# Attention of a two-layer trunk: low weight parts made by adding transfers, softmax weights transposed on row halves

## The chip, the cores and the metric

The kernel runs on one core of a Trainium2 chip. The metric is the time on the device of one execution, in microseconds; times before and after are medians of several runs. The engines are named as in the profile: PE (TensorE) with its weight loads PEld, DVE (VectorE), ACT (ScalarE), POOL (GpSimd) and SP (SyncE, which issues most transfers).

## The reference

Two layers work on 256 latent tokens and 256 context tokens, each with 1024 channels, in float32. What matters here is the token-mixing half of a layer:

```python
h  = modulate(rmsnorm(x,  norm1_g[l]), sh1,  sc1)      # latent
hc = modulate(rmsnorm(xc, norm1_g[l]), csh1, csc1)     # context
p  = h @ w_in[l]       # conv branch | q | k | v | gates
pc = hc @ w_in[l]      # in the last layer only its k and v
q, k = rope_2d(q), rope_2d(k)
y_conv = conv_branch(p[..., :GLU_END], ...)            # GLU, 31 taps, LayerNorm, swish, projection
s = concat(window scores + bias, context scores)       # 8 heads of 64
y_attn = (softmax(s) @ [v_win, v_ctx]) @ w_na_out[l]
x = x + g1 * gated_merge(p[..., QKV_END:], y_conv, y_attn, w_out[l])
```

In the first layer the context tokens go through the same steps and attend to context alone. A gated MLP with a convolution of width 3 follows in each layer, and the output is the latent stream after a last RMSNorm.

## The kernel before

Activations lie with channels on the 128 partitions and tokens along the free dimension: 512 columns (latent, context) in the first layer, 256 in most of the second. To keep float32 accuracy with TensorE's faster float32r type, every operand is split into a high part, rounded to float32r, and a low part, the rest. A product is then three matmuls (`mm3`, L179 to L181): high weight by high activation, high weight by low activation, low weight by high activation. The low part of a weight is needed only by the third.

Weights come in units of 128 x 1024 numbers (512 KB), eight 128 x 128 blocks each. `wunit` loads a unit into a `raw` buffer by a transfer that SP issues (L157), ACT copies it to `whi` (L160), and DVE subtracts the two into `wlo` (L161). `raw`, `whi` and `wlo` have four buffers each, so a unit can be made ready while three others wait or are in use. `unit8` returns a unit as eight pairs for `group`, which makes one output tile of 128 channels from eight blocks, that is 24 matmuls.

In the first layer the order of units in the input projection is: queries and keys of head pair 0 (units 6 and 10 of `U_IN`), then for each of the pairs 1 to 3 two units of the convolution's GLU and the pair's queries and keys, then gates from unit 14 on. In the second layer GLU units 0 and 1 come first, then four units of values, units 2 and 3, the first pair, 4 and 5, and then gates alternate with the other pairs.

Attention runs beside this. `group` calls `slot`, and a slot lets side work take a step: convolution taps on DVE, and `Attention.step`. A step does up to three things in PE's order: `turn` transposes the softmax weights that the step before left (16 transposes of 128 x 128; L494 for latent queries, L499 for context ones) and has ACT copy each of four PSUM banks to `pT` (L495, L500); `values` multiplies `V` with an earlier `pT` (L512); `products` makes the next scores (L440), on 64 rows of the array for each of the two heads of a pair. DVE then adds bias and takes the maximum (L458), and ACT does the exponential and the scaling (L461, L464). PSUM banks come under the names `sc` (two), `pt`, `po` and `main` (four); a turn and the scores after it use the same `sc`, `pt` and `main`.

The engines run their queues in order. The order in each queue is fixed when the program is built, from program order and when data and buffers are expected; `issue_after` adds orders by hand.

Of the kernel before, what the change touches and what calls it, by code (L numbers as in the profile page):

```python
# [8 lines left out]
F32 = mybir.dt.float32  # L9
F32R = mybir.dt.float32r  # L10
BF16 = mybir.dt.bfloat16
AF = mybir.ActivationFunctionType
ALU = mybir.AluOpType
AX = mybir.AxisListType

P = 128
# [3 lines left out]
S = 256  # L20
# [11 lines left out]
UW = 1024  # L32
LAT, CTX = slice(0, S), slice(S, 2 * S)
# [3 lines left out]

U_GLU0, U_V, U_IN, U_NA, U_CO, U_WO, U_UP, U_DN = 0, 2, 6, 36, 40, 44, 52, 96
NU = 118
T_GLU, T_Q, T_K, T_GATE = 0, 6, 10, 14  # L40

SWAP16 = [(i + 16) % 32 for i in range(32)]
# [3 lines left out]
def trunk(ctx: ExitStack, tc: tile.TileContext, xt, cvec, crow, wall, wada, params, bias_t, rope_t, out):  # L46
    nc = tc.nc
# [12 lines left out]
    def nm(s):  # L60
        uid[0] += 1
        return f"{s}_{uid[0]}"
# [3 lines left out]
    def psum(tag="main"):  # L66
        return psp.tile([P, 512], F32, tag=tag, bufs=BANKS[tag], name=nm(tag))
# [7 lines left out]
    def sl(w, i):  # L75
        return w[:, i * P : (i + 1) * P]
# [29 lines left out]
    start = ExitStack()  # L106
# [38 lines left out]
    def raw_unit(src, r=None):  # L145
        r = wp.tile([P, UW], F32, tag="raw", bufs=4, name=nm("raw")) if r is None else r
        lastdma[0] = sp.dma_start(r, src)
        return r
# [21 lines left out]
    def wunit(l, u, at=None, cuts=1):  # L170
        w, more = wparts(l, u, at, cuts)
        more()
        return w
# [9 lines left out]
    def group(ps, ws, xh, xl, c):  # L183
# [6 lines left out]
        slot()  # L190
        return ps

    def unit8(l, u, at=None):
        w = wunit(l, u, at)
        return [cols(w, i) for i in range(KD)]


# [187 lines left out]
    class Attention:  # L385
# [99 lines left out]

        def turn(self, what, its, pps):

            pts = [self.eb.tile([P, 4, S], F32, tag="pT", bufs=4, name=nm("pT")) for _ in range(2)]
            for n, tags in enumerate((("sc", "sc"), ("pt", "main"))):
                for i, pp in enumerate(pps[n]):  # L490
                    pt = psum(tags[i])
                    if what == LAT:
                        for kt in range(4):
                            pe.transpose(sl(pt, kt), sl(pp, kt), ident)  # L494
                        act.copy(pts[i][:, :, n * P : (n + 1) * P], pt.rearrange("p (k q) -> p k q", k=4))  # L495
                    else:
                        for t in range(2):
                            for kt in range(2):
                                pe.transpose(pt[:, kt * S + t * P : kt * S + (t + 1) * P], sl(pp, 2 * t + kt), ident)  # L499
                        act.copy(pts[i][:, 2 * n : 2 * n + 2, :], pt.rearrange("p (k q) -> p k q", k=2))  # L500
            js = [its[0][0]] if what == LAT else [it[0] for it in its]
            self.pv.append((what, js, pts))

        def values(self, what, js, pts, bank):
            po = psum(bank)
            kts = range(4) if what == LAT else range(2, 4)
            for n, j in enumerate(js):
                c = slice(n * S, (n + 1) * S)
                for kt in kts:
                    for i in range(2):  # L510
                        h = 2 * j + i
                        pe.matmul(  # L512
                            po[i * HD : (i + 1) * HD, c], self.V[kt][:, h * HD : (h + 1) * HD],
                            pts[i][:, 2 * n + kt - kts[0], :], start=kt == kts[0], stop=kt == kts[-1],
                        )
            for n, j in enumerate(js):
                c = slice(n * S, (n + 1) * S)
                act.copy(self.oh[j][:, what], po[:, c])
                dve.tensor_tensor(self.ol[j][:, what], po[:, c], self.oh[j][:, what].bitcast(F32), ALU.subtract)
# [705 lines left out]
```

## Time and profile before

| | |
|---|---|
| median of 3 runs | 1127.9 us (1127.66 to 1128.62) |
| the profiled execution | 1127.64 us, span 1125.9 us |
| granted TensorE clock, mean | 0.998 |
| PE busy | 1114.1 us (99%) |
| PEld busy | 963.0 us (86%) |
| DVE busy | 908.3 us (81%) |
| ACT busy | 563.6 us (50%) |
| POOL busy | 14.7 us (1%) |

The attention of the first layer lies between about 82 and 199 us, that of the second between 797 and 867 us. A timeline line gives start in us, duration in us, engine, line, operation, the tile written and those read, the shape and how often it was merged; in square brackets stands idle time of the engine before it and what ended it. For matmuls the start-to-start distance is the pace; the durations overlap.

### The profile page before, as it was taken

To read this page: it belongs to the slowest core of one execution; us is meant where nothing else is said; L and a number is where in the kernel's file an instruction comes from. 1 tells how busy PE (TensorE), PEld (TensorE's weight loads), DVE (VectorE), ACT (ScalarE), POOL (GpSimd) and SP (SyncE) were. 2 spreads that over 40 slices of the span, in tenths; PEclk is the share of its full clock that TensorE was granted. 3 is DMA by queue.
4 is the path that set the end of the run, shared out by engine and by line. 5 is a ranking of instruction groups with operands and counts; after the bars stand their busy time and mean duration, and the time that the engine had idled before them with its cause. 6 is when DMAs were issued, how large, how long until landed. Compare 5 with 4: busy or idle time off the path is not lost.

```text
span 1125.9 us, 17731 instructions
## 1 busy us (share of the span) xinstructions
PE 1114.1 (99%) x6828; PEld 963.0 (86%) x6828; DVE 908.3 (81%) x1631; ACT 563.6 (50%) x934; POOL 14.7 (1%) x24
## 2 busy tenths in 40 slices
PE   9999999999999999999999999999999999999997
PEld 7778777787789988888888888989888999999997
DVE  5689999685778788888898555789996898988773
ACT  4347657542333543434343222544677667766642
POOL 0000000000000000000000000000000000000000
PEclk9999999999999999999999999999999999999999
DMA  9833231536734354554556665556433575565781
GB/s 364 282 94 103 75 118 38 206 97 214 245 118 138 114 161 150 168 169 149 168 171 215 219 191 186 180 181 187 145 126 121 167 250 163 188 194 181 219 268 58
DMA packets 53941, 190.83 MB, mean 169 GB/s; under 512 B 6240, under 2 KB 6496, under 8 KB 53856
## 3 DMA queue, kind: packets, MB, share of 16 engines
q1 hardware_dynamic: 53568, 189.65, 52.1%
q8 instruction: 54, 0.88, 0.3%
q14 instruction: 31, 0.25, 0.1%
q10 hardware_dynamic: 288, 0.04, 0.0%
HBM read 188.62 MB, written 1.05 MB: 168 GB/s over the span
## 4 chain that ended last, share of the span: by engine, by line
PE 83%; DVE 9%; issue 6%; ACT 2%; DMA 0%; POOL 0%; POOLq 0%; DVEq 0%; SPq 0%; ACTq 0%
PE main L179 24%; PE main L181 24%; PE main L180 24%; DVE cb L591 4%; PE main L644 4%; DVE wlo L161 1%; PE sc L181 1%; PE sc L179 1%; PE sc L180 1%; PE po L202 1%; PE po L512 1%; PE sc L129 1%; PE sc L440 0%; DMA sb<-in_crow 0%; PE sc L494 0%
## 5 line engine op out<-in xcount | busy, mean ns | idle before, releaser
L179 PE MATMUL main<-h,whi 128*128 128x256 f32 (+1 forms) x1328 | 446.7, 337 | 0.0
L181 PE MATMUL main<-h,wlo 128*128 128x256 f32 (+1 forms) x1328 | 442.9, 335 | 1.0 <-DVE wlo L161 1.0
L180 PE MATMUL main<-h,whi 128*128 128x256 f32 (+1 forms) x1328 | 442.2, 334 | 0.1
L160 ACT CAST whi<-raw 128x1024 fp32r<-128x1024 f32 (+1 forms) x244 | 252.3, 1039 | 285.5 <-PE main L180 131.5
L161 DVE TENSOR_TENSOR wlo<-raw,whi 128x1024 fp32r<-128x1024 f32 (+1 forms) x244 | 292.9, 1207 | 112.5 <-ACT whi L160 108.0
L179 PEld LDWEIGHTS main<-h,whi 128*128 128x128 f32 x1328 | 249.4, 188 | 32.1 <-issue 3.6
L181 PEld LDWEIGHTS main<-h,wlo 128*128 128x128 f32 x1328 | 249.3, 188 | 29.6 <-DVE wlo L161 1.5
L180 PEld LDWEIGHTS main<-h,whi 128*128 128x128 f32 x1328 | 249.8, 188 | 28.5 <-DVE h L367 0.5
L591 DVE SCALAR_TENSOR_TENSOR cb<-u,par,cb 128x512 f32<-128x512 f32 (+1 forms) x240 | 140.4, 609 | 1.4
L271 DVE CUSTOM_DVE_ANT_0 t<-raw,sb,par 128x1024 bf16<-128x1024 f32 x100 | 126.7, 1277 | 1.0 <-ACT sb L255 0.7
L179 PE MATMUL main<-fh,whi 128*128 128x256 f32 (+1 forms) x386 | 123.0, 319 | 0.0
L180 PE MATMUL main<-fl,whi 128*128 128x256 f32 (+1 forms) x386 | 122.9, 319 | 0.0
L181 PE MATMUL main<-fh,wlo 128*128 128x256 f32 (+1 forms) x386 | 122.9, 318 | 0.0
L180 PEld LDWEIGHTS main<-fl,whi 128*128 128x128 f32 x386 | 72.7, 188 | 5.6
L179 PEld LDWEIGHTS main<-fh,whi 128*128 128x128 f32 x386 | 72.7, 188 | 5.6
L181 PEld LDWEIGHTS main<-fh,wlo 128*128 128x128 f32 x386 | 72.7, 188 | 5.5
L963 ACT ACTIVATE t<-main,par 128x512 f32<-128x512 f32 (+1 forms) x82 | 50.6, 667 | 39.0 <-PE main L181 39.0
L964 DVE SCALAR_TENSOR_TENSOR t<-main,par,t 128x510 f32<-128x510 f32 (+1 forms) x82 | 47.5, 615 | 10.2 <-ACT t L963 9.8
L967 DVE SCALAR_TENSOR_TENSOR t<-main,par,t 128x510 f32<-128x510 f32 (+1 forms) x82 | 46.6, 609 | 0.0
L366 ACT ACTIVATE h<-t,mod 128x256 fp32r<-128x256 f32 x56 | 25.4, 502 | 36.1 <-DVE t L365 36.1
L898 DVE SCALAR_TENSOR_TENSOR x<-main,mod,x 128x256 f32<-128x256 f32 x48 | 22.1, 479 | 23.5 <-PE main L181 23.3
L644 PE MATMUL main<-whi,h 128*128 128x512 f32 x128 | 40.6, 402 | 0.1
(221 smaller groups left out, 1188.2 us busy)
## 6 DMA issues: line engine op xcount, KB each, us to landing
raw<-in_wall SPq DMA_DIRECT2D x239, 512.0 KB, 4.2
raw<-in_wada SPq DMA_DIRECT2D x88, 512.0 KB, 4.3
bias<-in_bias_t SPq DMA_DIRECT2D x8, 640.0 KB, 4.8
row<-in_wada SPq DMA_DIRECT2D x8, 512.0 KB, 4.7
sb<-in_crow SPq DMA_DIRECT2D x5, 512.0 KB, 6.0
x<-in_xt SPq DMA_DIRECT2D x8, 256.0 KB, 4.4
raw<-in_wall SPq DMA_DIRECT2D x8, 256.0 KB, 7.1
out<-t SPq DMA_DIRECT2D x3, 256.0 KB, 2.1
```

What stands on the lines that cost most here:

```text
L160: act.copy(hi[:, c], r[:, c])
L161: dve.tensor_tensor(lo[:, c], r[:, c], hi[:, c].bitcast(F32), ALU.subtract)
L179: pe.matmul(ps, w[0], xh, start=start, stop=False)
L180: pe.matmul(ps, w[0], xl, start=False, stop=False)
L181: pe.matmul(ps, w[1], xh, start=False, stop=stop)
L271: dve.tensor_tensor_reduce(tmp().bitcast(BF16), r, v, 1.0, pr(l, BADA + n, 1), ALU.mult, ALU.add, mods[l][:, n, s : s + 1])
L366: high = act.activation(hi[:, c], y[:, c], AF.Identity, bias=b)
L591: dve.scalar_tensor_tensor(cb[j], src, w, cb[j], ALU.mult, ALU.add)
L644: mm = pe.matmul(pv[t], h1[n == 1][k][:, c], w[n == 2][:, b], start=k + n == 0, stop=k == KD - 1 and n == 2)
L963: act.activation(c, pv_, AF.Identity, bias=pr(l, FDB + t, 1), scale=w[1])
L964: dve.scalar_tensor_tensor(c[:, :, 1:], pv_[:, :, : S - 1], w[0], c[:, :, 1:], ALU.mult, ALU.add)
L967: dve.scalar_tensor_tensor(c[:, :, : S - 1], pv_[:, :, 1:], w[2], c[:, :, : S - 1], ALU.mult, ALU.add)
```

## The change

For 19 units of the first layer's input projection (0 to 18 of `U_IN`) and 11 of the second's (1, 3, 5 to 9 and 14 to 17), `unit8` calls `wadded` in place of `wunit`. There ACT makes the high part as before and then writes its negative into `wlo`; a transfer that GpSimd issues adds `raw` to it. DVE has no part in these units any more.

In `turn`, each 128 x 128 transpose becomes two: of rows 0 to 63 and of rows 64 to 127 of the weights. Each gives 64 columns, and the two go to two PSUM banks, so that one bank holds one half of the queries for both heads. Both banks of a pair are taken before the first transpose, and the two copies by ACT follow the 16 transposes of the pair. `pT` becomes one tile for both heads with as many bytes as the two before. For context the order of blocks inside the loop is rearranged so that one loop serves both kinds.

The space reserved for the descriptors of GpSimd's transfers is set to 1024 bytes per partition.

```diff
+ADDED = {*((0, U_IN + i) for i in range(19)), *((1, U_IN + i) for i in (1, 3, 5, 6, 7, 8, 9, 14, 15, 16, 17))}
...
+    def wadded(l, u):
+
+        r = raw_unit(wall[l, u])
+        hi = wp.tile([P, UW], F32R, tag="whi", bufs=4, name=nm("whi"))
+        lo = wp.tile([P, UW], F32R, tag="wlo", bufs=4, name=nm("wlo"))
+        act.copy(hi, r)
+        act.mul(lo, hi.bitcast(F32), -1.0)
+        pool.dma_start(lo, r, accum_op=ALU.add)
+        return hi, lo
+
     def unit8(l, u, at=None):
-        w = wunit(l, u, at)
+        w = wadded(l, u) if (l, u) in ADDED else wunit(l, u, at)
         return [cols(w, i) for i in range(KD)]
...
         def turn(self, what, its, pps):
 
-            pts = [self.eb.tile([P, 4, S], F32, tag="pT", bufs=4, name=nm("pT")) for _ in range(2)]
+            pT = self.eb.tile([P, 2, 4, S], F32, tag="pT", bufs=2, name=nm("pT"))
             for n, tags in enumerate((("sc", "sc"), ("pt", "main"))):
+                outs = [psum(t).rearrange("p (i s q) -> p i s q", i=2, s=4) for t in tags]
                 for i, pp in enumerate(pps[n]):
-                    pt = psum(tags[i])
+                    for s in range(4):
+                        src = s if what == LAT else s % 2 * 2 + s // 2
+                        for pt, r in zip(outs, HALF):
+                            pe.transpose(pt[:, i, s], sl(pp, src)[r], ident[r, r])
+                for pt, r in zip(outs, HALF):
                     if what == LAT:
-                        for kt in range(4):
-                            pe.transpose(sl(pt, kt), sl(pp, kt), ident)
-                        act.copy(pts[i][:, :, n * P : (n + 1) * P], pt.rearrange("p (k q) -> p k q", k=4))
+                        act.copy(pT[:, :, :, n * P + r.start : n * P + r.stop], pt)
                     else:
-                        for t in range(2):
-                            for kt in range(2):
-                                pe.transpose(pt[:, kt * S + t * P : kt * S + (t + 1) * P], sl(pp, 2 * t + kt), ident)
-                        act.copy(pts[i][:, 2 * n : 2 * n + 2, :], pt.rearrange("p (k q) -> p k q", k=2))
+                        to = pT[:, :, 2 * n : 2 * n + 2].rearrange("p i k (t q) -> p i (k t) q", t=2)
+                        act.copy(to[:, :, :, r], pt)
...
-                            pts[i][:, 2 * n + kt - kts[0], :], start=kt == kts[0], stop=kt == kts[-1],
+                            pT[:, i, 2 * n + kt - kts[0]], start=kt == kts[0], stop=kt == kts[-1],
...
-    nc = bacc.Bacc("TRN2", target_bir_lowering=False, num_devices=1)
+    nc = bacc.Bacc("TRN2", target_bir_lowering=False, num_devices=1, dynamic_dma_scratch_size=1024)
```

More of the change, by code (lines that the diff above doesn't have):

```diff
@@ L486, in turn, with values @@
         def turn(self, what, its, pps):
-            pts = [self.eb.tile([P, 4, S], F32, tag="pT", bufs=4, name=nm("pT")) for _ in range(2)]
+            pT = self.eb.tile([P, 2, 4, S], F32, tag="pT", bufs=2, name=nm("pT"))
             for n, tags in enumerate((("sc", "sc"), ("pt", "main"))):
+                outs = [psum(t).rearrange("p (i s q) -> p i s q", i=2, s=4) for t in tags]
                 for i, pp in enumerate(pps[n]):
-                    pt = psum(tags[i])
+                    for s in range(4):
[3 more added lines that the diff above has]
+                for pt, r in zip(outs, HALF):
                     if what == LAT:
-                        for kt in range(4):
-                            pe.transpose(sl(pt, kt), sl(pp, kt), ident)
-                        act.copy(pts[i][:, :, n * P : (n + 1) * P], pt.rearrange("p (k q) -> p k q", k=4))
-                    else:
-                        for t in range(2):
-                            for kt in range(2):
-                                pe.transpose(pt[:, kt * S + t * P : kt * S + (t + 1) * P], sl(pp, 2 * t + kt), ident)
-                        act.copy(pts[i][:, 2 * n : 2 * n + 2, :], pt.rearrange("p (k q) -> p k q", k=2))
+                        act.copy(pT[:, :, :, n * P + r.start : n * P + r.stop], pt)
+                    else:
+                        to = pT[:, :, 2 * n : 2 * n + 2].rearrange("p i k (t q) -> p i (k t) q", t=2)
+                        act.copy(to[:, :, :, r], pt)
             js = [its[0][0]] if what == LAT else [it[0] for it in its]
-            self.pv.append((what, js, pts))
-        def values(self, what, js, pts, bank):
+            self.pv.append((what, js, pT))
+        def values(self, what, js, pT, bank):
             po = psum(bank)
```

## The prediction

> **What bounds the kernel now.** I read the page's busy times first, then who waited for whom, then single stretches of the timeline.
>
> ```profile
> PE 1114.1 (99%) x6828; PEld 963.0 (86%) x6828; DVE 908.3 (81%) x1631; ACT 563.6 (50%) x934; POOL 14.7 (1%) x24
> ```
> ```profile
> PE main L181 <- DVE wlo L161: 1.0, 2, 0.6
> PE pt L1094 <- DVE t L314: 0.7, 1, 0.7
> ...
> PE pt L228 <- ACT t L221: 0.6, 1, 0.6
> ```
> ```profile
> 100.00:200.00 100.00, 100.00 (x572) 78.62 (x571) 99.46 (x191) 72.29 (x152) 2.99 (x2) 1.00 0.27 82
> 743.00:796.00 53.00, 53.00 (x315) 46.72 (x314) 52.93 (x115) 22.34 (x33) 0.00 (x0) 1.00 0.52 157
> ```
> The first row alone would not prove a PE bound, because matmul ends are modelled. The waits do: in the whole span PE waited 1.0 us for low parts (first of these rows: total, times, longest). The last two rows are the attention of the first layer and the start of that of the second; their columns are window, length, then busy us of PE, PEld, DVE, ACT, POOL, the granted clock (1.00), DMA share and GB/s. DVE is full there (99.46 of 100, 52.93 of 53), and yet PE has no idle time. So DVE is full without holding anything up: its low parts run far ahead of the matmuls that read them. Time can only be won here by shortening PE's own work.
>
> **The low parts.** Removed: 30 subtractions on DVE (19 in the first layer, 11 in the second). Added: 30 negated copies on ACT and 30 transfers issued by GpSimd.
>
> ```profile
> L161 DVE TENSOR_TENSOR wlo<-raw,whi 128x1024 fp32r<-128x1024 f32 x238 | 288.8, 1220 | 112.2 <-ACT whi L160 108.0 <-PE sc L181 3.2 <-PE sc L440 0.3
> ...
> L160 ACT CAST whi<-raw 128x1024 fp32r<-128x1024 f32 x238 | 248.8, 1050 | 285.5 <-PE main L180 131.5 <-DMA raw<-in_wall 128.7 <-issue 11.8
> ```
> DVE loses 30 x 1.22 = 36.6 us. By the waits above PE gets at most 1.0 us of that, and I count none. ACT gains 30 x 1.05 = 31.5 us (the negated copy has the shape of the high part's copy); if 14 of them fall between 100 and 200, ACT goes from 72.3 to 87 of 100 us. The price for PE is whether the low part still comes in time. Budgets are read from the end of the high part's copy to the first L181 that reads the unit:
>
> ```profile
> 733.27 1.05 ACT L160 CAST whi<-raw 128x1024 fp32r<-128x1024 f32 x1 [3.56 <-DMA raw<-in_wall]
> ```
> ```profile
> 740.60 0.28 PE L181 MATMUL main<-h,wlo 128*128 128x256 f32 x1
> ```
> ```profile
> 760.18 1.05 ACT L160 CAST whi<-raw 128x1024 fp32r<-128x1024 f32 x1 [1.74 <-PE main L644]
> ```
> ```profile
> 768.81 0.28 PE L181 MATMUL main<-h,wlo 128*128 128x256 f32 x1
> ```
> ```profile
> 779.85 1.05 ACT L160 CAST whi<-raw 128x1024 fp32r<-128x1024 f32 x1 [0.37 <-PE main L180]
> ```
> ```profile
> 788.59 0.28 PE L181 MATMUL main<-h,wlo 128*128 128x256 f32 x1
> ```
> These are units 1, 3 and 7 of the second layer's input projection. After the high part there are 740.60-734.32 = 6.3 us, 768.81-761.23 = 7.6 us and 788.59-780.90 = 7.7 us. The negated copy takes 1.05 of each, so a transfer may take X = 5.2, 6.5 and 6.6 us from issue to landing. Units of 512 columns run 5.6 us each (24 matmuls at the 0.23 us spacing shown below), so with four buffers the first layer has about 3 x 5.6 - 2.1 = 14.7 us left after both copies, and I count no stall in it.
>
> No such transfer is in the trace. Its bounds are the nearest loads of the same 512 KB:
>
> ```profile
> raw<-in_wall SPq DMA_DIRECT2D x239, 512.0 KB, 4.2
> ...
> sb<-in_crow SPq DMA_DIRECT2D x5, 512.0 KB, 6.0
> ```
> A load reads once and writes once; the adding transfer reads source and destination and writes, and GpSimd must issue it. At 4.2 us nothing stalls; at 6.0 unit 1 stalls 0.8. If the doubled reading doubles the 4.2, X is 8.4. I take X = 5.5, nearer to the two rows than to the doubling: unit 1 stalls PE 5.5-5.2 = **+0.3 us**, the others fit. A gain below zero is excluded, since no wait of PE sits here. The Trainium skill ("DMA: Bandwidth & Descriptors", section "Anatomy of one DMA") gives for a GpSimd transfer 2.0 us plus bytes over 436 GB/s, as an estimate 3.2 us for 512 KB; by it the stall is 0, and no row here shows one to compare.
>
> The raw buffer is now held until the transfer lands. SP's queue is in order, so the load four units on, with all loads behind it, starts up to X later than the subtraction let it; in the first layer the buffer no longer waits for DVE's turn, which gives some of this back. I count nothing, covered by the spare above. The smaller descriptor space shifts addresses and adds no instruction: nothing.
>
> **The turned softmax weights.** Ten times in the kernel (eight latent steps, two of context) 16 transposes stand between the projections and what follows:
>
> ```profile
> 824.32 0.39 PE L180 MATMUL main<-h,whi 128*128 128x512 f32 x1
> 824.55 0.39 PE L181 MATMUL main<-h,wlo 128*128 128x512 f32 x1
> 824.79 1.03 PE L494 MATMUL sc<-ident,pp 128*128 128x128 f32 x8
> 825.66 0.60 PE L494 MATMUL pt<-ident,pp 128*128 128x128 f32 x4
> 826.09 0.60 PE L494 MATMUL main<-ident,pp 128*128 128x128 f32 x4
> 826.62 1.95 PE L512 MATMUL po<-pT,V 128*64 128x256 f32 x16
> 828.50 0.96 PE L440 MATMUL sc<-qk,qk 64*128 64x512 f32 x6
> ```
> Eight transposes start within 825.66-824.79 = 0.87 us: 109 ns each, and the block lasts 826.62-824.79 = 1.83 us. They are replaced by 32 on 64 rows, in pairs on the two halves of the array. Do pairs overlap? The values' 16 matmuls of 256 columns, in pairs on column halves, take 828.50-826.62 = 1.88 us, 235 ns per pair; one after the other at the transposes' 109/128 = 0.85 ns per column they would need 16 x 218 = 3.5 us. So halves do run side by side. What limits a pair is the identity's 64 columns, 64 x 0.85 = 54 ns, or the load of its weights:
>
> ```profile
> L494 PEld LDWEIGHTS sc<-ident,pp x64: 138/141/144, 100.5 to 856.1; 128*128 128x128 f32 x64
> ```
> ```profile
> L512 PEld LDWEIGHTS po<-pT,V x144: 132/137/138, 111.8 to 866.4; 128*64 128x64 f32 x144
> ```
> ```profile
> L202 PEld LDWEIGHTS po<-raw,sil x128: 105/109/111, 10.5 to 49.7; 128*32 128x32 f32 x128
> ```
> From 32 to 64 columns a load grows by 28 ns, so about 81 ns are latency, and the transposes' load of 128 columns occupies 141-81 = 60 ns. A pair is thus 54 to 60 ns if loads too run side by side, 109 if the load or the issue of twice the instructions holds it at the old pace. I take 58, from the two rows it is nearest to: 16 x (109-58) = 0.82 us won per block.
>
> Against it stands a change of array shape that was not there before, priced from where PE goes from 128 to 64 rows today:
>
> ```profile
> 81.67 0.39 PE L180 MATMUL main<-h,whi 128*128 128x512 f32 x1
> 81.90 0.40 PE L181 MATMUL main<-h,wlo 128*128 128x512 f32 x1
> 82.23 0.97 PE L440 MATMUL sc<-qk,qk 64*128 64x512 f32 x6
> ```
> The step into 64 rows is 0.33 us instead of 0.23, and the three pairs last 0.97 instead of 2 x 0.23 + 0.39 = 0.85: 0.10 + 0.12, so 0.2 us. The way out to the values cost a change before and costs one after. The Trainium skill ("TensorEngine Tiling (Array Packing)", section "Key Properties") speaks against the edit here: a change of tiling mode, not of tile alone, drains TensorE. The trace agrees (0.33 against 0.23).
> Net **0.82 - 0.20 = 0.62 us** per block, where PE's next work is free to start. That is not so in three blocks:
>
> ```profile
> 101.60 1.06 ACT L495 COPY pT<-sc 128x512 f32<-128x512 f32 x2
> ```
> ```profile
> 102.52 1.16 PE L440 MATMUL sc<-qk,qk 64*128 64x512 f32 x6
> ```
> ```profile
> 112.81 1.07 ACT L495 COPY pT<-sc 128x512 f32<-128x512 f32 x2
> ```
> ```profile
> 113.70 1.21 PE L440 MATMUL sc<-qk,qk 64*128 64x256 f32 x12
> ```
> In the first block of a layer no values follow; the next scores need the two sc banks, which ACT frees at 102.66, and they already take 1.16 us instead of 0.96. In the block at 110 ACT frees them at 113.88, just when the scores start. These three win nothing. The other seven win 7 x 0.62 = **-4.3 us**. Their cover: copies on ACT start 0.9 us after the block, as the timeline of the usual case shows, and end 2.95 us after it:
>
> ```profile
> 825.71 1.06 ACT L495 COPY pT<-sc 128x512 f32<-128x512 f32 x2
> 826.66 0.60 ACT L495 COPY pT<-pt 128x512 f32<-128x512 f32 x1
> 827.13 0.61 ACT L495 COPY pT<-main 128x512 f32<-128x512 f32 x1
> ```
> Now both banks of a pair fill together, so a copy waits for eight pairs instead of four transposes: 0.2 + 8 x 0.058 = 0.66 against 4 x 0.109 = 0.44 us, still ahead of the 0.92 at which ACT comes free of the high part's copy. With the block at 1.2 us the scores start at 1.2 + 1.88 = 3.1 on sc (copied at 1.98) and 0.8 later on pt and main (2.95). One negated copy in front is hidden; two pieces cost about 1 us.
>
> **Sum.** -4.3 + 0.3 = -4.0 us. The profiled execution took 1127.64 us (span 1125.9 and 1.74 around it) and lies 0.26 under the median 1127.9. So 1127.64 - 4.0 + 0.26 = **1123.9 us**.
>
> **Rivals.**
> 1. *The adding transfers are long, and PE waits for low parts: slower.* With X the stalls are (X-5.2)+(X-6.5)+(X-6.6); they eat the 4.3 at X = 7.5, and at X = 9 they are 8.7, so 1127.9 - 4.3 + 8.7 = 1132.3. For it: three operands, GpSimd's issue, DMA share 0.52 where the second layer starts. Against: loads of 4.2 and 6.0. Chance 0.21.
> 2. *The pairs do not shorten the block.* At 109 ns a pair the change of shape alone is left: 7 x 0.2 + 0.3 = +1.7, 1129.6. Against: the values overlap. Chance 0.09.
> 3. *ACT turns late.* Two extra pieces ahead of the copies cost 1 us in about half of the blocks and eat most of the gain: 1123.9 + 3 = 1127. For it: 87 of 100 us busy, and the block at 110. Chance 0.08.
> 4. *GpSimd's queue is blocked.*
>
> ```profile
> POOL ss L842 <- DVE cb L591: 193.8, 2, 135.3
> ```
> GpSimd sat 135.3 us on one sum of convolutions. Transfers queued behind such a wait come too late by whatever exceeds their budget of some 15 us; 10 us gives 1134. Against: those sums stand later in the program. Chance 0.05.
>
> **Numbers.** Forecast 0.57. A measurement can tell 0.2%, 2.3 us, from no change. Faster (under 1125.6): the forecast, 0.57. Same: rivals 2 and 3, 0.17. Slower: rivals 1 and 4, 0.26. Low end: pairs of 52 ns win in eight blocks 8 x 0.71 = 5.7 us, and the 1.0 us of waits partly goes: 1121.5. High end: rival 1 at X = 9, 1132.0; about 0.15 lies above it, the rest of 0.2 below the low end. The forecast's own range is 1121.5 to 1125.6.
>
> **What would show it.** Right: blocks of transposes of about 1.2 us instead of 1.83, each beginning 0.33 us after the last projection matmul starts; DVE's busy time down by some 37 us and ACT's up by 31, neither with an effect on PE; PE's waits for low parts at most about 1 us more; transfers landing within 5 to 6 us. Wrong: blocks still of 1.8 us; a row of PE waiting for a GpSimd transfer of several us near 741, 769 or 789; scores after a block held by the copies of L495's successor.

## The result, and the profile after

The changed kernel takes **1135.4 us** (median of 4 runs, 1133.3 to 1136.8) against 1127.9 us before: ratio **1.0065, 95% interval 1.0053 to 1.0077**. The medians lie 7.5 us apart (by the ratio 7.3), where 4.0 us less were forecast. The profiled execution of it took 1134.42 us, span 1132.6.

The page's busy times of the changed kernel:

```profile
PE 1114.0 (98%) x6988; PEld 957.7 (85%) x6988; DVE 881.6 (78%) x1601; ACT 592.2 (52%) x964; POOL 41.0 (4%) x54
```

VectorE lost 26.7 us of busy time and ScalarE gained 28.6. PE is busy as long as before, but the span is 6.7 us longer: PE waits, or works at a lower clock. Who waited for whom (total us, times, longest), the rows that before did not have:

```profile
PE main L182 <- DMA wlo<-raw: 3.4, 2, 2.6
PE sc L451 <- ACT pT L509: 2.1, 4, 0.8
...
PE pt L506 <- ACT pp L493: 1.8, 1, 1.8
```

To see where the time went, I compared the two traces step by step. The projections of both kernels hold the same matmuls, so the start of every eighth of them (L179 before, L180 after) can be set against its partner: 166 pairs. The table shows by how much the distance after minus before grew over each stretch, in us; the columns are named after the time before (in us) at which the stretch has its block of transposes or its wait. The stretch "units 13-17" also holds the block at 825 us. "Start" is the offset with which the comparison begins and belongs to no step. All kernels of the experiments are in it, in the order in which they are told below.

```
             start first  110  133-  190   209  unit 1 unit 7 first units 841,  rest  sum without
                   block       176              of L2  of L2  of L2 13-17 855        start
after        -0.1  +0.9   0.0  -1.0  +5.0  -0.8  +2.8   +1.1  +0.9  -0.1  -1.2  -0.4   +7.2
rows          0.0   0.0  +0.6  -1.8  +1.6  +3.5   0.0    0.0  +0.5   0.0  -0.9  +0.2   +3.7
added        -0.2   0.0  +0.1   0.0  +2.4  -0.2  +1.6   +0.9   0.0  +1.0   0.0  +0.9   +6.7
rows_l0      +0.3  +0.9   0.0  -1.0  +2.4  -0.2   0.0    0.0  +0.2   0.0  -0.9  +0.2   +1.5
rows_l1      +0.4   0.0  +0.6  -1.8  +3.3  -0.2  +4.0   +0.6  +0.9  -0.1  -1.2  -0.5   +5.4
whole190     +0.7   0.0  +0.6  -1.8  +1.6  +1.0   0.0    0.0  +0.6   0.0  -0.9  +0.3   +1.4
ada_dve      +0.4   0.0  +0.6  -1.8  +1.6  -0.8   0.0    0.0  +0.1   0.0  -0.9  +0.2   -1.0
fill190      +1.1  +0.9   0.0  -1.0  +3.2  -0.8  +4.4   +0.5  +0.9  -0.1  -1.2  -0.5   +6.1
less         -0.4   0.0  +0.3  +0.1  +3.5  -0.8   0.0    0.0  +0.7  +0.8  -1.2  -0.3   +3.2
hold_after   +1.1  +0.9   0.0  -1.8  -0.6  -0.8  +2.4   +0.6  +0.9  +3.4  -1.2  -0.4   +3.3
hold_rows    -0.1   0.0  +0.6  -1.8  -0.6  -0.8   0.0    0.0  +0.1   0.0  -0.9  +0.3   -3.1
best         +0.3   0.0  +0.6  -1.8  -0.6  -0.6   0.0    0.0  +0.1   0.0  -0.9  -0.1   -3.3
best_l0       0.0   0.0  +0.3  -1.0  -0.6  -0.8  +0.1    0.0  +0.1   0.0  -0.9  -0.2   -3.0
```

In the row of the changed kernel the blocks that were meant to gain do gain (-0.6 each at 133, 160, 841 and 855). Most of the loss sits in five places: the block at 190 us, units 1 and 7, and the first block of each layer. The largest is the last context turn of the first layer, at 190 us. These are the timelines of PE there, before and after:

```profile
190.49 1.03 PE L499 MATMUL sc<-ident,pp 128*128 128x128 f32 x8
191.36 0.60 PE L499 MATMUL pt<-ident,pp 128*128 128x128 f32 x4
191.80 0.60 PE L499 MATMUL main<-ident,pp 128*128 128x128 f32 x4
192.33 0.87 PE L512 MATMUL po<-pT,V 128*64 128x256 f32 x6
```
```profile
190.38 0.78 PE L506 MATMUL sc<-ident,pp 64*128 64x64 f32 x16
192.98 0.32 PE L506 MATMUL pt<-ident,pp 64*128 64x64 f32 x1 [1.82 <-ACT pp L493]
...
194.68 2.83 PE L524 MATMUL po<-pT,V 128*64 128x256 f32 x12
```

The first half of the block is short (0.78 us). Then PE waits 1.82 us for weights that ScalarE has yet to scale. The block ends at 194.68 instead of 192.33. ScalarE itself was late, because VectorE's maxima were. Before and after, the first exponential of this step:

```profile
184.09 0.47 ACT L477 ACTIVATE pp<-sc,mx 128x256 f32<-128x256 f32 x1 [3.21 <-DVE mx L472]
```
```profile
187.19 0.48 ACT L488 ACTIVATE pp<-sc,mx 128x256 f32<-128x256 f32 x1 [5.79 <-DVE mx L483]
...
192.40 1.72 ACT L493 ACTIVATE pp<-pp,ri 128x256 f32<-128x256 f32 x4
```

The last of these lines is the last scaling, which ends at 194.1 us. The first exponential starts 3.1 us later than before, and ScalarE idled 5.79 us in front of it. VectorE was not idle meanwhile; it worked off other things that stand ahead of the maxima in its queue, a low part and convolution taps:

```profile
182.10 1.22 DVE L162 TENSOR_TENSOR wlo<-raw,whi 128x1024 fp32r<-128x1024 f32 x1
183.24 2.32 DVE L603 SCALAR_TENSOR_TENSOR cb<-u,par,cb 128x512 f32<-128x512 f32 x3
185.47 0.42 DVE L531 TENSOR_TENSOR ol<-po,oh 128x256 fp32r<-128x256 f32 x1
185.81 0.74 DVE L603 SCALAR_TENSOR_TENSOR cb<-u,par,cb 128x512 f32<-128x512 f32 x1
186.47 1.28 DVE L483 TENSOR_REDUCE mx<-sc 128x2 f32<-128x512 f32 x2
```

The timelines of VectorE show where its freed time went: 116 of the first layer's 120 taps run ahead of these maxima, where in the kernel before it was 97.

And the wait has a sequel. In the windows after it (busy us of PE, PEld, DVE, ACT, POOL, then the granted clock, DMA share, GB/s) the clock is 0.51, and VectorE has nothing to do:

```profile
189.00:193.00 4.00, 2.18 (x25) 1.50 (x23) 3.82 (x9) 4.00 (x16) 0.00 (x0) 1.00 0.00 0
193.00:196.00 3.00, 2.90 (x22) 1.86 (x24) 0.03 (x1) 2.97 (x6) 0.00 (x0) 0.51 0.00 0
196.00:200.00 4.00, 4.00 (x16) 2.37 (x13) 0.00 (x0) 4.00 (x9) 0.00 (x0) 0.51 0.00 0
```

The second kind of loss is unit 1 of the second layer. GpSimd issues its adding transfer, PE stops before the first matmul that reads the low part, and the view of the tile `wlo` gives the spread of all 30 transfers:

```profile
738.25 0.93 POOL L201 DMA_DIRECT2D wlo<-raw  x1 [1.29 <-ACT t L329]
```
```profile
744.58 0.28 PE L181 MATMUL main<-h,whi 128*128 128x256 f32 x1
747.43 0.39 PE L182 MATMUL main<-h,wlo 128*128 128x256 f32 x1 [2.58 <-DMA wlo<-raw]
```
```profile
DMA to landing us min/median/max: 4.4/5.7/9.1
```

The transfer that landed at 747.4 is the slowest of the 30: 747.4 - 738.25 = 9.1 us. Unit 7 loses 1.1 us in the same way.

The third kind of loss is the first block of each layer, +0.9 us in both. In the first layer ScalarE's queue reads: high part, negated copy, and only then the copies that free the banks for the scores; PE waits 0.81 us:

```profile
100.55 1.05 ACT L199 CAST whi<-raw 128x1024 fp32r<-128x1024 f32 x1 [1.93 <-PE main L181]
101.62 1.06 ACT L200 ACTIVATE wlo<-whi 128x1024 fp32r<-128x1024 f32 x1
102.59 1.06 ACT L509 COPY pT<-sc 128x512 f32<-128x512 f32 x2
```
```profile
103.21 0.99 PE L451 MATMUL sc<-qk,qk 64*128 64x512 f32 x4 [0.81 <-ACT pT L509]
```

The second layer's first block shows the same queue and a wait of 0.80 us. But not all of its 0.9 belongs to the negated copy: in the kernels below that have no transfer in layer 2, this stretch grows by 0.1 to 0.6 us too.

### The profile page after: what moved, and what is told of

The parts are those of the page before. It is cut to its first block, busy times and chain, and to the rows that moved or that the text cites. A ratio compares the mean times of both kernels' runs of the same rounds, so it can differ in the third digit from the quotient of the medians.

```text
span 1132.6 us, 18142 instructions
## 1 busy us (share of the span) xinstructions
PE 1114.0 (98%) x6988; PEld 957.7 (85%) x6988; DVE 881.6 (78%) x1601; ACT 592.2 (52%) x964; POOL 41.0 (4%) x54
## 4 chain that ended last, share of the span: by engine, by line
PE 83%; DVE 10%; ACT 3%; DMA 2%; issue 1%; SPq 0%; DVEq 0%; ACTq 0%
PE main L180 24%; PE main L182 24%; PE main L181 24%; DVE cb L603 6%; PE main L656 3%; DMA wlo<-raw 1%; PE po L524 1%; PE sc L180 1%; PE sc L182 1%; PE sc L181 1%; DVE wlo L162 1%; PE po L213 1%; ACT whi L161 1%; PE sc L451 1%; DMA x<-in_xt 1%
## 5 line engine op out<-in xcount | busy, mean ns | idle before, releaser
L180 PE MATMUL main<-h,whi 128*128 128x256 f32 (+1 forms) x1328 | 447.0, 337 | 0.0
L162 DVE TENSOR_TENSOR wlo<-raw,whi 128x1024 fp32r<-128x1024 f32 (+1 forms) x214 | 256.9, 1207 | 132.4 <-ACT whi L161 131.3
L161 ACT CAST whi<-raw 128x1024 fp32r<-128x1024 f32 (+1 forms) x214 | 221.1, 1038 | 250.3 <-DMA raw<-in_wall 121.9
L180 PEld LDWEIGHTS main<-h,whi 128*128 128x128 f32 x1328 | 249.7, 188 | 32.6 <-issue 4.3
L603 DVE SCALAR_TENSOR_TENSOR cb<-u,par,cb 128x512 f32<-128x512 f32 (+1 forms) x240 | 143.6, 623 | 2.4
L180 PE MATMUL main<-fh,whi 128*128 128x256 f32 (+1 forms) x386 | 123.0, 319 | 0.0
L180 PEld LDWEIGHTS main<-fh,whi 128*128 128x128 f32 x386 | 72.7, 188 | 5.6
L199 ACT CAST whi<-raw 128x1024 fp32r<-128x1024 f32 x30 | 31.5, 1049 | 28.7 <-PE main L181 20.0
```

The lines of the kernel that those rows point to most:

```text
L161: act.copy(hi[:, c], r[:, c])
L162: dve.tensor_tensor(lo[:, c], r[:, c], hi[:, c].bitcast(F32), ALU.subtract)
L180: pe.matmul(ps, w[0], xh, start=start, stop=False)
L199: act.copy(hi, r)
L603: dve.scalar_tensor_tensor(cb[j], src, w, cb[j], ALU.mult, ALU.add)
```

## The experiments

**The parts alone.** Four kernels, each timed beside before on the same chip (before 1127.8 us). Theory A: the halves gain as forecast and all loss is the transfers'. Theory B: the halves cost something themselves. (For `added` the letters stand for something else: A for late maxima and late landings, B for late landings alone.)

`rows`, the halves without any adding transfer:

```diff
-ADDED = {...}
+ADDED = set()
-    nc = bacc.Bacc(..., dynamic_dma_scratch_size=1024)
+    nc = bacc.Bacc(...)
```


> Only the transposes on row halves; every low part made on DVE as before. Theory A (the halves win about 0.6 us per block, the loss comes from what the adding transfers do to the queues): the block at 190 us does not wait long, five to seven blocks win 0.6 to 0.7 us, 1123.0 to 1124.8 us. Theory B (the halves themselves cost, because both banks of a pair now need both heads' weights and their copies end together): the last context block of the first layer waits and the clock drops as in the changed kernel, 1127 us or more.

`added`, the 30 transfers with the turn of before:

```diff
-            pT = self.eb.tile([P, 2, 4, S], ...)
...
+            pts = [self.eb.tile([P, 4, S], ...) for _ in range(2)]
+            ... whole transposes, copies by head, as before
```


> Only the adding transfers (30 units) with the smaller descriptor space; transposes whole as before. Theory A: the maxima of the last context scores of the first layer still come about 3 us late on DVE, PE waits near 190 us, its clock drops (+5), units 1 and 7 of the second layer come late (+3.9): 1136 to 1138 us. Theory B: only the late transfers are left, 1131 to 1132 us.

`rows_l0` and `rows_l1`, the halves with the transfers of one layer:

```diff
-ADDED = {*((0, U_IN + i) for i in range(19)), *((1, U_IN + i) for i in (1, 3, 5, ...))}
+ADDED = {*((0, U_IN + i) for i in range(19))}                 # rows_l0
+ADDED = {*((1, U_IN + i) for i in (1, 3, 5, ...))}            # rows_l1
```


> Row halves, and adding transfers in the first layer alone (19 units). Theory A: +4.0 us by the end of the first layer as in the changed kernel, then three or four blocks of the second layer win 0.6 each: 1129.5 to 1130.5 us. Theory B: the same first layer; second layer not better than before, 1132 us.

> Row halves, and adding transfers in the second layer alone (11 units). Theory A: the first layer wins 2.4 to 3 us, the second loses 3 (2.8 for unit 1, 1.0 for unit 7, 0.9 for copies behind a negated copy, less three blocks): 1128 to 1129 us. Theory B: the first layer loses 4 as in the changed kernel: 1135 us.

Measured: `rows` 1130.5 us (1.0021, 1.0011 to 1.0030), `added` 1133.3 (1.0056, 1.0039 to 1.0074), `rows_l0` 1130.5 (1.0021, 1.0012 to 1.0031), `rows_l1` 1132.9 (1.0043, 1.0028 to 1.0058). Theory A falls with `rows`: the halves alone make the kernel slower. Theory B has that sign right, and its figures fit none of the other three. `rows_l0` comes out at the upper end of its theory A (1129.5 to 1130.5), but by luck: the first layer costs 2.1 us by the table where 4.0 were expected, and the second layer gains less. In `rows` the steady blocks gain as they should, -1.8 for three, and then PE gives it all back at 190 us (+1.6) and at 209 us (+3.5).

`added` separates two things. PE saves nothing there ahead of 190 us, and still it loses 2.4 us at that place: as in the change, 116 taps run ahead of the maxima, and the exponentials start at 187.32. So the transfers make the maxima late without any help from the halves. The same count parts all kernels in which no taps are held back: 115 or 116 with the transfers of layer 1, 97 or 98 without. Its theory A had said that the maxima come late; the time is under that theory's 1136 to 1138, and in this profile the clock stays up at 190 us. Its steps at units 1, 7 and 13-17 are late landings, three waits of 2.8 us in all. The two waits of `rows` that before had shorter or not at all:

```profile
PE pt L239 <- ACT t L232: 2.6, 1, 2.6
...
PE pt L506 <- ACT pp L493: 1.2, 1, 1.2
```

At 209 us PE turns rows that ScalarE copies (L232); in ScalarE's queue the copy stands behind the activations of two loads of `in_crow`, one of which landed at 210.5. Before and in `rows`:

```profile
207.15 2.01 ACT L255 ACTIVATE sb<-sb 128x1024 f32<-128x1024 f32 x2
209.06 0.35 ACT L221 COPY t<-sc 128x256 f32<-128x256 f32 x1
```
```profile
207.93 1.06 ACT L266 ACTIVATE sb<-sb 128x1024 f32<-128x1024 f32 x1
210.47 1.06 ACT L266 ACTIVATE sb<-sb 128x1024 f32<-128x1024 f32 x1 [1.49 <-DMA sb<-in_crow]
211.44 0.35 ACT L232 COPY t<-sc 128x256 f32<-128x256 f32 x1
```

So the new theory M: at 190 and at 209 us what PE needs had been ready only just in time. PE time saved ahead of such a place turns into waiting there, so does any lateness of the other engines, and a long wait halves the clock for some microseconds more. The transfers then add their own: a late landing, and shifts of order in VectorE's and ScalarE's queues. At 209 us it is lateness alone: by the table PE comes there 0.4 us later in `rows` than before, and the copy 2.4 us later, because the second load was issued 1.3 us later (202.06 against 200.73) and took 8.4 us to land.

**Is it the pairs, the clock, the copy?** Four kernels more (before 1128.1 us).

`whole190`: `rows` with whole transposes in the last context turn of layer 1.

```diff
+                if what == CTX and not self.todo:
+                    ... whole transposes head by head, a copy for each, as before
+                    continue
```


> The row halves alone (median 1130.5 us), with whole transposes head by head, as before, in the last context turn of layer 1. Theory M (the maxima of that turn come about 1.3 us later on VectorE than before, and TensorE comes 1.2 us earlier, so the last normalised weights end at 192.2 us whichever way they are turned): TensorE still waits 1 to 2 us inside that block, the turn ends within 0.3 us of where it ended, time 1130.2 to 1130.8. Theory H (a pair of halves needs both heads' weights, where a whole transpose needs one): the wait inside the block falls below 0.4 us and the step of +1.6 us there goes away, time about 1128.8.

Measured 1129.7 us (1.0017, 1.0008 to 1.0027), between the two expectations, so the trace has to decide. PE still waits in mid-block, and the step there is +1.64 as in `rows` (+1.63):

```profile
190.01 1.03 PE L498 MATMUL sc<-ident,pp 128*128 128x128 f32 x8
191.94 0.83 PE L498 MATMUL pt<-ident,pp 128*128 128x128 f32 x4 [0.89 <-ACT pp L487]
192.73 0.84 PE L498 MATMUL main<-ident,pp 128*128 128x128 f32 x4
```

The wait is the lateness of the weights, not the pairing. In this profile the wait at 209 us was 1.6 us long instead of 2.6 and the clock stayed up, which is where it is ahead of `rows`. The other runs fit that: the mean granted clock is 0.998 in seven of its ten runs and in one of the ten of `rows`.

`ada_dve`: `rows` with that one copy on VectorE.

```diff
-        lastev[0] = act.copy(ev, ps[:, :S])
+        lastev[0] = dve.tensor_copy(ev, ps[:, :S]) if now else act.copy(ev, ps[:, :S])
...
-            ev = ada_rows(ada_products(l, j, "sc"))
+            ev = ada_rows(ada_products(l, j, "sc"), (l, j) == (0, 8))
```


> The row halves alone (median 1130.5 us), with the copy of the rows that the transposes at about 209 us turn taken from ScalarE, where it stands behind the activations of in_crow, to VectorE. Theory G (TensorE waits 2.6 us there for the copy, and the clock that it is granted falls to half because of the wait): both go, the step of +3.45 us there becomes -0.2 to -0.8, time 1126.7 to 1127.3. Theory C (the clock falls for another reason than the wait): the wait goes, about 1.2 us come back over before's 0.7 us of idle time, and a stretch of 0.5 stays at 209 to 218 us; time 1128.5 to 1129.3.

Measured 1128.4 us (1.0005, 0.9996 to 1.0015): 2.1 us under `rows`, no different from before. The wait and the low clock are gone and the step is -0.8, as theory G said; the median lies 1 us above what it expected. The profiled run is not a typical one: it took 1126.97 us with a mean clock of 0.998, and the only other run with that clock took 1126.78, both inside theory G's range. Six of the others have 0.996, two 0.997. A stretch of 3.4 us at half clock takes 0.0015 off the mean, so most of the runs probably had one that the profiled run escaped; no trace shows where. The wait at 190 us (1.1 us in this profile) is still there.

`fill190`: the whole change, with work that nobody reads in the gap at 190 us.

```diff
+                if n == 1 and what == CTX and not self.todo:
+                    free = psum("po")
+                    for _ in range(8):
+                        pe.matmul(sl(free, 0), ident, ident, start=True, stop=True)
```


> The change as it is (1135.4 us), with eight multiplications of the identity that nobody reads, 128x128 each, put before the second half of the last context turn of layer 1, where TensorE stood idle for 1.8 us. They do nothing but fill the wait. Theory G (the granted clock halves for about 6.7 us because TensorE stood idle): the clock stays over 0.9 between 193 and 200 us, the block takes about 3.5 us and the values 1.9 instead of 4.30 and 3.61, time 1131.7 to 1132.7. Theory C (the clock falls for another reason): 0.5 stays there, time 1135 to 1136.

```profile
189.00:193.00 4.00, 4.00 (x35) 3.17 (x34) 3.85 (x8) 4.00 (x16) 0.00 (x0) 1.00 0.00 0
193.00:196.00 3.00, 2.85 (x32) 2.18 (x32) 1.11 (x4) 2.98 (x10) 0.00 (x0) 1.00 0.00 0
196.00:200.00 4.00, 4.00 (x27) 2.81 (x24) 0.00 (x0) 3.99 (x7) 0.00 (x0) 1.00 0.00 0
```

The clock stays at 1.00, so the low clock came from PE standing idle. The step shrinks by 1.9 us, from +5.0 to +3.2, where I expected 2.7 to 3.7 less time, because the weights are still late and the copies behind them (PE waits 0.6 us for those of L512) come next. Some 2 of the 5.0 us at 190 us are thus the low clock's, most of the rest is the wait. Measured 1133.9 us (1.0055, 1.0040 to 1.0070), between the two expectations: that idle time lowers the clock is shown in the trace, and the time alone would not show it.

`less`: the change without four of the 30 transfers, which VectorE subtracts again.

```diff
-ADDED = {*((0, U_IN + i) for i in range(19)), *((1, U_IN + i) for i in (1, 3, 5, 6, 7, 8, 9, 14, 15, 16, 17))}
+ADDED = {*((0, U_IN + i) for i in range(19) if i != 4), *((1, U_IN + i) for i in (3, 5, 6, 8, 9, 14, 15, 16))}
```


> The change without four of its 30 adding transfers: unit 4 of layer 1 and units 1, 7 and 17 of layer 2, which VectorE subtracts again. Theory P (the transfers cost where one lands late, units 1 and 7 with 2.8 and 1.1 us, and where a negated copy stands before the first copies of the turned weights, units 4 and 17 with 0.9 us each; the other 26 cost little by themselves): time 1129.5 to 1131. Theory E (each transfer costs about the same, (1135.4 - 1130.5)/30 = 0.16 us, by its traffic or its place in the queues): time 1134.5 to 1135.

Measured 1131.5 us (1.0033, 1.0021 to 1.0045), 0.5 above theory P's range and 3 us below theory E's. The stalls of units 1 and 7 and the +0.9 of the very first block are gone. The first block of layer 2 still has +0.7: another unit's negated copy (at 811.81) now stands ahead of its first copies. The transfer of that same unit lands late, which costs 0.8 us:

```profile
PE main L182 <- DMA wlo<-raw: 1.1, 1, 1.1
```

Why the blocks up to 176 us gain nothing here (+0.1) is open.

**The cause at 190 us.** Three kernels, in which VectorE takes its work in another order (before 1127.8 us). The last taps of the first layer's convolution may only start when the context maxima are taken.

```diff
-                dve.tensor_reduce(mx, ...)
+                self.mx = dve.tensor_reduce(mx, ...)
...
-                                conv_tap(*taps.pop(0))
+                                with tc.issue_after(att.mx.ins) if not last and len(taps) <= 28 else ExitStack():
+                                    conv_tap(*taps.pop(0))
```


> The change as it is (1135.4 us), with the last 28 taps of layer 1's convolution held back on VectorE until the last context maxima of that layer are taken. No instruction is added or left out; only VectorE's order is another. Theory M (the 5.0 us lost at 190 us come from maxima that stand behind taps and low parts on VectorE, 3.1 us later than before): the maxima are taken 3 to 5 us earlier, TensorE's wait of 1.8 us inside the block goes, the granted clock stays at 1.00, and the step there becomes -0.6 us; time 1129.8 to 1130.8. Theory B (the wait only moves: the taps held back end late and the normalisation behind them then keeps TensorE waiting at 205 to 260 us): at least 2 us of the gain come back there; time 1132 or more.

This is `hold_after`, the whole change with that edit. Measured **1128.8 us** (1.0012, 1.0001 to 1.0023; runs from 1126.2 to 1132.8), 6.6 us under the change as it is and 1 us under what theory M expected. VectorE takes the maxima at 181.58 instead of 186.47, and PE has no gap and no low clock left there:

```profile
181.58 1.29 DVE L482 TENSOR_REDUCE mx<-sc 128x2 f32<-128x512 f32 x2
```
```profile
189.00:193.00 4.00, 4.00 (x50) 2.97 (x50) 3.82 (x6) 3.97 (x7) 0.00 (x0) 1.00 0.00 0
193.00:196.00 3.00, 3.00 (x18) 2.12 (x15) 2.86 (x5) 3.00 (x7) 0.00 (x0) 1.00 0.00 0
```

The step is -0.6 as in any other block, and nothing is given back at 209 us or behind. Theory M is shown for this place, theory B falls. What keeps this kernel from a gain are late landings, worse in this profile than in that of the change (three waits, 4.7 us; behind one of them the clock halves at 822.9 us, +3.4 in all); that they differ from execution to execution fits the wide range of its times.

```profile
PE main L182 <- DMA wlo<-raw: 4.7, 3, 2.2
```

`hold_rows` is `ada_dve` with the same edit (26 taps), and `best` sums the last values of layer 2 in `sc`:

```diff
-                self.values(*work, "sc" if work[0] == CTX and not (soft or self.todo) else "po")
+                self.values(*work, "sc" if not (soft or self.todo) else "po")
```


> The row halves alone with the copy for the transposes at 209 us on VectorE (median 1128.4 us), and the last 26 taps of layer 1 held back on VectorE until the last context maxima are taken. Theory M: the step of +1.6 us at 190 us becomes -0.6, time 1126.0 to 1126.6, faster than before. Theory B (the wait moves behind the taps): 1127.5 or more.

> The last kernel with one more edit: the last turn's values of layer 2 are summed in a bank of sc, not in po, for which TensorE waits 0.7 us until VectorE has read the values before. Theory M: another -0.7 us, time 1125.3 to 1126.0, faster than before by 0.15 to 0.25%. Rival (the values' bank was not what TensorE waited for; it waits for the copies that ScalarE makes of the turned weights): no gain over the last kernel, 1126.0 to 1126.6.

Measured `hold_rows` 1125.3 us (0.9977, 0.9968 to 0.9987) and `best` **1124.4 us (0.9971, 0.9961 to 0.9982)**. Both are faster than before and than the change, and lower than expected by 0.7 and 0.9 us. With the two chains out of the way these kernels gain 2.5 and 3.4 us, where the prediction had priced 4.3 for the halves: by the table of `hold_rows` five of its seven blocks bring the whole 0.6 (133, 160, 176, 190 and 841), the one at 855 half of it and the one at 825 nothing. The bank of `best` seems to add something: the intervals overlap, but of the 72 pairs of one run of each, `best` is the faster in 62. The wait for `po` is gone from its trace and the stretch behind 857 us is 0.4 us shorter.

**The transfers where they do no harm.** `best_l0` puts 18 of layer 1's transfers into `best` (before 1128.2 us); 28 taps are held instead of 26.

```diff
-ADDED = set()
+ADDED = {(0, U_IN + i) for i in range(19) if i != 4}
```


> The last kernel (1124.4 us: row halves, taps held, the copy at 209 us on VectorE, the last values in sc) with 18 of layer 1's 19 adding transfers put back (all but unit 4, whose negated copy stood before the first copies), none in layer 2, and 28 taps held. Theory M (transfers cost only where one lands late or shifts a queue that TensorE is about to wait for, and VectorE's freed time buys nothing, since TensorE waits for VectorE nowhere in that stage): no late landing in layer 1, so within 0.6 us of the last kernel, 1124.0 to 1125.2. Theory E (each transfer costs 0.1 to 0.2 us whatever its place): 1126.2 to 1128. Theory V (VectorE's relief is worth something there, the wait of 0.55 us at the second block among them): 1123.0 to 1124.0.

Measured 1124.8 us (0.9971, 0.9960 to 0.9981): the same as `best`, theory M. VectorE's busy time is 16.5 us less (893.6 against 910.1) and ScalarE's 16.6 more (579.8 against 563.2), and neither moves the end.

Not tried: the transfers in layer 2 with an earlier issue, and the smaller descriptor space by itself. `best_l0` has the larger space that the kernel before has, and its transfers land within 5.7 us in the median and 8.2 at most; with the smaller one those of `rows_l0` take 5.6 and 8.4. So the space makes no difference that these two show.

## Why the prediction was wrong

**The step that failed is "The other seven win 7 x 0.62", with what it rests on: "DVE is full without holding anything up", and its relief counted as nothing.** The price of a block was right: entry 0.33 us, pairs 62 ns apart where 58 were forecast, a block of 834.02 to 835.17 = 1.15 us where 1.2 was forecast, and -0.58 to -0.62 in every block whose next work is free. That 58 came so near is in part luck: the working by weight loads gives 28 ns for 32 more columns, and its own rows give 4 ns for the 64 after those (137 to 141).

```profile
833.69 0.40 PE L182 MATMUL main<-h,wlo 128*128 128x512 f32 x1
834.02 0.71 PE L506 MATMUL sc<-ident,pp 64*128 64x64 f32 x16
...
835.17 1.95 PE L524 MATMUL po<-pT,V 128*64 128x256 f32 x16
```

What failed is the reading behind it. "PE has no idle time" was taken to mean that nothing else was near. Windows and waits show a wait of zero in the same way whether the lead is 10 us or 0.5. The lead stood in the timeline before, and the prediction did not read it: ScalarE's last scaling of the step at 190 us ended at 189.30 + 1.72 = 191.0,

```profile
189.30 1.72 ACT L482 ACTIVATE pp<-pp,ri 128x256 f32<-128x256 f32 x4
190.90 0.59 ACT L628 COPY g<-main 128x512 f32<-128x512 f32 x1
```

and PE began to turn these weights (`main`) at 191.80. That is a lead of 0.8 us, and the weights hang on VectorE's maxima. In the change PE comes to this block only 0.1 us earlier than before (190.38 against 190.49), so it is not time saved on PE that is given back there. The weights come 3.1 us later, because VectorE took up its freed time with taps ahead of the maxima. One sum accounts for nine kernels: how much later than before the last scaling ends, less the lead of 0.8, against how far PE is behind the kernel before at the first projection matmul that was compared after the block (us, "start" included):

```
                    rows  ada_dve whole190 added rows_l0   rows_l1 less  after fill190
weights later       +1.3   +1.7    +2.1    +3.2   +3.5      +1.7   +3.3  +3.1   +4.2
less the lead       +0.5   +0.9    +1.3    +2.4   +2.7      +0.9   +2.5  +2.3   +3.4
PE behind by        +0.4   +0.8    +1.2    +2.3   +2.6      +2.4   +3.6  +4.8   +4.1
```

In the first five the clock stays up, and the sum comes out within 0.2 us. In the next three it halves, and they lose 1.1 to 2.5 us more; `fill190` waits 0.6 us for copies. In `rows`, without any transfer, PE had come 1.2 us earlier and the weights 1.3 us later: there both count.

My block at 190 us was to bring -0.62 and cost +5.0: 5.6 of the 11.2 us between the forecast -4.0 and the +7.2 of the trace. `hold_after` shows the cause: with the maxima taken earlier the same block wins its 0.6.

**The transfers' X = 5.5 us.** The median was right (5.7), but a stall is not set by the median. Unit 1, with the smallest budget, drew 9.1. Units 1 and 7 cost 3.9 us where 0.3 was counted. In the four other profiles that have this transfer it takes 6.6 to 8.8 us and PE waits 1.4 to 2.6 for it, so it was not one unlucky draw; why it always lands later than the median is open. This is the mechanism of the first rival, which ended on the right side with chance 0.21; by its own formula X = 9 gave 1132.3 (the prediction's high end says 1132.0). It is the second largest term, not the cause.

**"One negated copy in front is hidden."** True in blocks that values follow. In the first block of a layer no values follow, so there is no cover, and these blocks cost 0.9 us each (in the second layer not all by the copy, as said). The prediction had named exactly these blocks as winning nothing and then asked only whether they would gain. That is 1.7 us. The block at 110 us won nothing, as forecast; without transfers in layer 1 it even loses 0.6, where the scores wait for ScalarE's copies (0.85 us in `rows`).

**DVE and ACT.** -26.7 and +28.6 where -36.6 and +31.5 were forecast. The work was priced rightly: the subtractions fall from 288.8 to 252.8 us, by 36.0. The busy total falls by less, since what is left overlaps less and the taps take longer. The total does not bear on the end, as `best_l0` shows. That they would be "neither with an effect on PE" was right for the load and wrong for the order: the maxima moved behind taps that nobody needed yet. No term of the sum priced order.

**Rivals 2 to 4.** The pairs shorten the block, so 2 falls. ScalarE's copies were late (3) in four blocks, by 0.8 us in the first of each layer and by 0.2 to 0.3 at 110 and 176 us, and not in half of those that were to win. GpSimd's queue was not blocked (4): it issued about 0.4 us after each negated copy ended (0.30 to 0.42).

The rest of the 11.2 us: 0.8 at 176 us, where the scores wait for late copies, and 0.5 at 825 us, where the block wins little. Against it stand 0.8 us at 209 us and 0.5 behind 930 us: waits of 0.6 and 0.4 us that before had there are gone in the change.

## What to carry to other kernels

Before counting a saving on the engine that never waits, go down its timeline and read at each place where it takes another engine's result how long that result had been ready; the saving counts only up to the smallest of these leads, summed over all savings ahead of it, and lateness of the other engine beyond the lead is paid in full. Before counting relief of an engine as harmless, ask what will fill the freed time, and whether it comes ahead of a result that is needed soon. Where a lead is too short, look at what stands ahead of the late instruction in its own engine's queue: here holding back taps that nobody was waiting for took 6.6 us off the change, and turned the halves from no difference into a gain of 2.5 us, with not one instruction fewer. A transfer on a path with a few us of spare must be judged by its slowest landing, not its median.

## What the runs showed of the hardware

**The clock gate.** The trace's records of the granted clock change only in steps of 3.41 us: `rows` drops to half at 211.64 for 3.41 us, the change at 193.07 for 6.83. I cut each trace into windows of 3413 ns from the first change to full clock and took the share of each without a matmul in flight. Up to about 1100 us the emptiest windows are these:

```
idle share  clock of the next window  kernel
0.69        half                      rows
0.68        half                      fill190
0.65        half                      hold_after
0.55        half                      rows_l1
0.53        half                      after
0.53        half                      less
0.48        full                      added
0.41        full                      after
0.41        half                      rows_l1
0.40        full                      whole190, added, hold_after
```

All six over one half were followed by half clock. Of those with 0.40 or less all but one were followed by full clock; the one is the first of the change's two windows at half clock (idle share 0.03), and why its stretch lasted two windows is open. Between 0.40 and one half it goes both ways. So a gap of 1.82 us is enough when it falls into one window, and one of 2.58 us (the change at 744.86) costs no clock when a boundary cuts it into 1.17 and 1.40. The price of the same wait thus depends on where the boundaries fall, and they fall elsewhere in each execution. The Trainium skill ("TensorE: Matmul & The Clock Gate", section "What's actually happening") states a free-running window of 3413 ns, and the trace agrees. The Trainium skill (the same page, section "Why this matters for your kernels") asks for no gaps over about 3 us; here gaps of 1.8 to 2.6 us were followed by half clock, and the measurement decides.

**Adding transfers.** For 512 KB between on-chip buffers 4.4 us at best, 5.7 in the median and 9.1 at most, and GpSimd is taken 862 to 1052 ns by each issue. In seven other profiles the median lay between 5.4 and 6.6 us and the slowest between 7.5 and 10.1. The Trainium skill ("DMA: Bandwidth & Descriptors", section "Anatomy of one DMA") had given 3.2 us as an estimate; no transfer here came near it.
